# Expert weights paired into 2 MB transfers of 16 KB rows, the expert sum kept in the stream's tile, gathered rows in a tile of their own

## The chip, the cores and the metric

The kernel runs on one core of one Trainium2 chip. The metric is the device time of one execution in microseconds (us). Within a profile, times count from the start of the profiled span.

## The reference

A two-layer backbone on 256 latent tokens of width 1024 (and 256 context tokens in the first layer), all in float32. Layer 0 is attention and a dense SwiGLU; layer 1 is a short gated convolution and the part that this case is about, a top-2-of-8 expert SwiGLU:

```python
logits = h @ router_w;  top_vals, top_idx = lax.top_k(logits, 2)
gates = sum(one_hot(top_idx, 8) * softmax(top_vals)[..., None])       # (tokens, 8)
out = sum over e of gates[..., e:e+1] * ((silu(h @ w_gate[e]) * (h @ w_up[e])) @ w_down[e])
x = x + g2 * out
```

Each expert has 3 x 1024 x 3584 float32 weights (44 MB), so all eight are 352 MB, three quarters of what the kernel reads from HBM.

## The kernel before

Weights are read as a list of *units* (`order`), each 1 MB: 128 partitions by 2048 floats, that is one row of 8 KB for each partition. Units go into 8 KB-per-partition buffers that are used in a ring (`ring`, `spare()` at line 62, `load()` at line 66); the DMA is issued on the SP queue (line 68). SP issues in program order, so a buffer that is not yet free holds up every load behind it. By the expert stage the ring has 13 buffers: five of `raw1`, three of `raw2`, three of `raw3`, one of `raw4`, one of `raw5`. Two more tiles take one unit each early on (`extra`): `xhat` takes the sixth expert unit and later becomes the expert sum `macc`, and `late` takes the eleventh and is then given to the output tiles `ys`.

An expert has 7 *chunks* of 512 hidden columns. A chunk takes six units: gate and up of the first half of the input, gate and up of the second half, and, one chunk later, two units of the down projection. Experts are ranked by their number of tokens. The four with the most are *heavy*: up to 128 rows, and each weight unit is split into a high and a low part (`parts`, lines 71 to 77: ScalarE writes `hi` at line 75, VectorE writes `lo` at line 76), which are multiplied in three float32r matmuls (`mac`, lines 305 to 309). The other four are *light*: up to 64 rows, units are used as they landed, by float32 matmuls on column pairs (`pair`, line 1371). The order of chunks (`chunks`, line 92) is four heavy ones, then heavy and light in turn, then four light ones at the end.

The helper `ahead` (line 141) asks for units up to eight ahead of the one in use, splitting heavy ones some parts early, in program order on ScalarE and VectorE; so these engines wait for a transfer before they go on to later work. Work around an expert's start and end is put at steps of a chunk by `hook(chunk, step, ...)` (from line 1405): `choice` compares token ranks with slots (line 1276), `slots` transposes that (line 1336), `fetch_rows` gathers the expert's token rows from the DRAM copy `xd` by an indirect DMA on the POOL queue (line 1284) into a ring buffer taken with `spare()`, `turn_rows` transposes them on TensorE (line 1298), `output` scales an expert's result and splits it into `yh` and `yl` (lines 1381 to 1384), `scatter` multiplies it by the one-hot rows (line 1391), and `scattered` adds it to `macc` (line 1398). The first expert takes its rows from `x` directly.

Of the kernel before, what the change touches and what calls it, by code (L numbers as in the profile page):

```python
# [15 lines left out]
D = 1024  # L16
# [18 lines left out]
def trunk(ctx, tc, i, out, dbg=None):  # L35
# [10 lines left out]
    small = ctx.enter_context(pool("small", 2))  # L46
    raw1 = ctx.enter_context(pool("raw1", 5))
    cur = {}
# [10 lines left out]

    ring = [raw1] * 5  # L60

    def spare():
        ring.append(ring.pop(0))
        return ring[-1].tile([128, 2048], F32, name="raw")

# [28 lines left out]

    def weights(m, r, c, h):
        def ap():
            if r and r not in who:
                who[r] = nc.values_load(cur["who"][0:1, r:r + 1], engines=[mybir.EngineType.SP], min_val=0, max_val=NE - 1)
            return i[m][who[r] if r else 0, c, h]
        return ap  # L100

    whole += [False] * len(order)
    for n in range(len(chunks) + 1):
        if n < len(chunks):
            order += [weights(m, *chunks[n], h) for h in range(2) for m in ("moe_g", "moe_u")]
            whole += [chunks[n][0] >= NE - NL] * 4
        if n:
            order += [weights("moe_d", *chunks[n - 1], h) for h in range(2)]
            whole += [chunks[n - 1][0] >= NE - NL] * 2
# [6 lines left out]
    ready, at, used = {}, [0, None], [0]  # L116

    def feed(upto):
        while at[0] <= min(upto, most[0]):
            u, h = divmod(at[0], 2)  # L120
            if h == 0:
                src = order[u]() if callable(order[u]) else order[u]
                if u in extra:
                    at[1] = extra.pop(u)()
                    sp.dma_start(at[1], src)
                else:
                    at[1] = load(src)
# [868 lines left out]
    ph = mctx.enter_context(pool("ph", 2))  # L996
    raw2 = ctx.enter_context(pool("raw2", 3, side="right"))
    m1 = ctx.enter_context(pool("m1", 1, side="right"))
# [4 lines left out]
    dump("x1", x)  # L1003
    ring[:0] = [raw2] * 3

# [39 lines left out]

    extra[FIRST + 5] = lambda: mp.tile([128, NT, D], F32, name="xhat").rearrange("p t d -> p (t d)")

# [16 lines left out]
    for j in range(4):  # L1064
# [23 lines left out]
        if j == 3:  # L1088
            late.close()
            raw3 = ctx.enter_context(pool("raw3", 3, side="right"))  # L1090
            raw4 = ctx.enter_context(pool("raw4", 1, side="right"))
            lp = late.enter_context(pool("late", 1, side="right"))

            def join(p):
                ring.append(p)
                return p.tile([128, 2048], F32, name="raw")
# [95 lines left out]
    mctx.close()  # L1192
    raw5 = ctx.enter_context(pool("raw5", 1))
    ring += [raw5]
    me = ctx.enter_context(pool("me", 2))
# [177 lines left out]
    def output(E, q):  # L1373

        if "y" not in cur:
            late.close()
            cur["y"] = ctx.enter_context(pool("ys", 2, side="right"))
# [15 lines left out]
    def scattered(E, q, t):  # L1393
        c = slice(512 * q, 512 * q + 512)
        if "macc" not in cur:
            cur["macc"] = mp.tile([128, NT, D], F32, name="xhat")
# [13 lines left out]
    for r, E in enumerate(experts):  # L1410
# [113 lines left out]

    macc = cur["macc"]
    for s in range(4):
        down(last, s)
    y = raw1.tile([128, 2048], F32, name="raw")[:, 0:512]
    dve.scalar_tensor_tensor(y, E.accs[0], E.gs, g2l, op0=OP.mult, op1=OP.mult)
# [4 lines left out]
    for t in range(NT):  # L1534
        for q in range(2):
            c = slice(512 * q, 512 * q + 512)
            dve.tensor_add(macc[:, t, c], macc[:, t, c], ends[q, t])
            sp.dma_start(out[t * 128:(t + 1) * 128, c], macc[:, t, c])

# [4 lines left out]
    with tc.If(flag > 0):  # L1544
        spill(tc, i, out, load, pm, acc, me, m1, x, macc, rs, am, bm, pos, gts, cap, g2, iota, ident)


def spill(tc, i, out, load, pm, acc, me, m1, x, macc, rs, am, bm, pos, gts, cap, g2, iota, ident):
    nc = tc.nc
    pe, act, dve, sp = nc.tensor, nc.scalar, nc.vector, nc.sync  # L1550
    p2 = m1.tile([128, NT, NE], F32, name="p2")
    for t in range(NT):
        dve.tensor_sub(p2[:, t], pos[:, t], cap)
    for e in range(NE):
# [18 lines left out]
        for c in range(NFC):  # L1573
            pg, pu = pm(), pm()
            for half in range(2):
                for n, p in (("moe_g", pg), ("moe_u", pu)):
                    w = load(i[n][e, c, half])
                    for k in range(4):
# [10 lines left out]
            for half in range(2):  # L1589
                w = load(i["moe_d"][e, c, half])  # L1590
                for s in range(2):
# [48 lines left out]
def layout(x, c, ctx, c_ctx, ada_w, ada_b, norm1_g, norm2_g, attn_w_in, attn_w_out, qnorm_a, knorm_a, qnorm_b,  # L1640
# [37 lines left out]
    a["conv_o"] = tall(conv_w_out[0])  # L1678
    for n, w in (("moe_g", moe_w_gate), ("moe_u", moe_w_up)):
        w = np.asarray(w).reshape(NE, 2, 4, 128, NFC, FC).transpose(0, 4, 1, 3, 2, 5)  # L1680
        a[n] = A(w).reshape(NE, NFC, 2, 128, 2048)
    w = np.asarray(moe_w_down).reshape(NE, NFC, 2, 2, 128, D).transpose(0, 1, 2, 4, 3, 5)
    a["moe_d"] = A(w).reshape(NE, NFC, 2, 128, 2048)
    return a
# [15 lines left out]
```

## Time and profile before

| | |
|---|---|
| median of 3 runs | 1363.53 us (1361.49 to 1364.81) |
| the profiled execution | 1361.22 us, of which the span is 1359.4 us |
| PE (TensorE matmul) busy | 1310.8 us, 96% |
| VectorE busy | 858.4 us, 63% |
| ScalarE busy | 700.8 us, 52% |
| mean granted clock of TensorE | 0.993 of full speed |
| DMA | 473.37 MB, mean 348 GB/s over the span |

A busy PE is not a PE at its peak, since matmuls overlap. The DMA share in a row of the stretches is the mean busy share of the 16 DMA engines; a little over 1 means that their packets overlap. The expert stage runs from about 490 us to the end.

### The profile page before, as it was taken

How to read it: one execution, taken by the hardware profiler on the slowest of the kernel's cores; microseconds unless marked ns; L12 is line 12 of the kernel's file. 1: busy time of each engine (PE TensorE's matmuls, PEld its weight loads, DVE VectorE, ACT ScalarE, POOL GpSimd, SP SyncE). 2: the span in 40 equal slices, each digit the busy share in tenths (PEclk: the TensorE clock that was granted, in tenths of full speed). 3: DMA queues.
4: the chain of work that ended last, by engine and by line, in shares of the span. 5: the costliest groups of instructions: out<-in, count | busy, mean ns of one | idle time of the engine just before them, and what ended most of it. 6: DMA issues, size and time to landing. Idle time of an engine off the chain costs nothing.

```text
span 1359.4 us, 19330 instructions
## 1 busy us (share of the span) xinstructions
PE 1310.8 (96%) x7328; PEld 916.1 (67%) x7328; DVE 858.4 (63%) x1164; ACT 700.8 (52%) x975; POOL 8.2 (1%) x13
## 2 busy tenths in 40 slices
PE   6998999999999999999999999999999999999997
PEld 4766789999989987865556656655556656655532
DVE  4777758577768669865655565565555565556421
ACT  5566765444464258855545544654444644554410
POOL 0000000000000000000000000000000000000000
PEclk9999999999999989999999999999999999999999
DMA  9833769678749469699999999999999999999996
GB/s 378 293 124 101 276 268 351 244 279 310 279 171 338 174 269 385 255 422 420 420 421 420 409 421 421 404 420 420 421 404 421 407 422 419 420 408 421 421 419 254
DMA packets 67091, 473.37 MB, mean 348 GB/s; under 512 B 7472, under 2 KB 8112, under 8 KB 11056
## 3 DMA queue, kind: packets, MB, share of 16 engines
q1 hardware_dynamic: 66240, 469.46, 86.1%
q0 software_dynamic: 752, 2.62, 0.6%
q8 instruction: 59, 0.97, 0.3%
q14 instruction: 40, 0.33, 0.1%
HBM read 469.95 MB, written 2.10 MB: 347 GB/s over the span
## 4 chain that ended last, share of the span: by engine, by line
PE 78%; DMA 9%; DVE 6%; ACT 4%; issue 2%; SPq 0%; ACTq 0%; DVEq 0%
PE pm L1371 14%; DMA raw<-in_moe_g_dram 7%; PE acc L305 6%; PE acc L307 6%; PE acc L309 6%; PE pm L305 5%; PE pm L307 5%; PE pm L309 5%; PE acc L1371 5%; PE pm L961 4%; PE pm L963 4%; PE pm L962 4%; DVE lo L76 3%; DMA raw<-in_moe_d_dram 2%; PE pm L1351 2%
## 5 line engine op out<-in xcount | busy, mean ns | idle before, releaser
L76 DVE TENSOR_TENSOR lo<-raw,hi 128x1024 fp32r<-128x1024 f32 x438 | 524.8, 1223 | 180.5 <-ACT hi L75 163.0
L75 ACT ACTIVATE hi<-raw 128x1024 fp32r<-128x1024 f32 x438 | 452.8, 1058 | 251.7 <-DMA raw<-in_moe_d_dram 75.5
L1371 PE MATMUL pm<-raw,hl 128*64 128x512 f32 x896 | 207.5, 600 | 3.5 <-DVE xhat L1398 3.2
L305 PE MATMUL pm<-hi,eh 128*128 128x512 f32 x448 | 179.0, 400 | 0.2 <-ACT g L291 0.2
L307 PE MATMUL pm<-lo,eh 128*128 128x512 f32 x448 | 175.5, 392 | 2.1 <-DVE lo L76 2.0
L309 PE MATMUL pm<-hi,el 128*128 128x512 f32 x448 | 174.6, 390 | 0.0
L1371 PEld LDWEIGHTS pm<-raw,hl 128*64 128x64 f32 x896 | 60.3, 137 | 116.1 <-issue 108.2
L963 PE MATMUL pm<-th,lo 128*128 128x256 f32 x480 | 135.9, 283 | 0.0
L962 PE MATMUL pm<-tl,hi 128*128 128x256 f32 x480 | 135.6, 283 | 0.0
L961 PE MATMUL pm<-th,hi 128*128 128x256 f32 x480 | 135.6, 283 | 0.0
L1371 PE MATMUL acc<-raw,dT 128*64 128x512 f32 x448 | 103.9, 599 | 0.0
L307 PEld LDWEIGHTS pm<-lo,eh 128*128 128x128 f32 x448 | 84.2, 188 | 20.5 <-DVE lo L76 4.5
L305 PEld LDWEIGHTS pm<-hi,eh 128*128 128x128 f32 x448 | 84.1, 188 | 19.8 <-issue 0.7
L1365 DVE TENSOR_TENSOR sg<-pm,sg 128x512 f32<-128x512 f32 (+1 forms) x56 | 38.6, 690 | 92.4 <-ACT sg L1364 92.1
L309 PEld LDWEIGHTS pm<-hi,el 128*128 128x128 f32 x448 | 84.1, 188 | 17.8
L961 PEld LDWEIGHTS pm<-th,hi 128*128 128x128 f32 x480 | 91.2, 190 | 0.8 <-issue 0.4
L962 PEld LDWEIGHTS pm<-tl,hi 128*128 128x128 f32 x480 | 91.0, 190 | 0.4
L963 PEld LDWEIGHTS pm<-th,lo 128*128 128x128 f32 x480 | 91.1, 190 | 0.0
L1364 ACT ACTIVATE sg<-pm 128x512 f32<-128x512 f32 (+1 forms) x56 | 32.8, 586 | 99.4 <-PE pm L1371 97.1
L305 PE MATMUL acc<-hi,dh 128*128 128x512 f32 x224 | 72.2, 403 | 0.0
L307 PE MATMUL acc<-lo,dh 128*128 128x512 f32 x224 | 69.3, 391 | 0.0
L309 PE MATMUL acc<-hi,dl 128*128 128x512 f32 x224 | 69.1, 390 | 0.0
(331 smaller groups left out, 1525.0 us busy)
## 6 DMA issues: line engine op xcount, KB each, us to landing
raw<-in_moe_d_dram SPq DMA_DIRECT2D x112, 1024.0 KB, 14.4
raw<-in_moe_g_dram SPq DMA_DIRECT2D x111, 1024.0 KB, 14.4
raw<-in_moe_u_dram SPq DMA_DIRECT2D x111, 1024.0 KB, 14.3
raw<-in_ada_w_dram SPq DMA_DIRECT2D x48, 1024.0 KB, 6.4
raw<-in_conv_i_dram SPq DMA_DIRECT2D x12, 1024.0 KB, 6.9
raw<-in_ffn_g_dram SPq DMA_DIRECT2D x11, 1024.0 KB, 6.8
raw<-in_ffn_u_dram SPq DMA_DIRECT2D x11, 1024.0 KB, 4.9
raw<-in_ffn_d_dram SPq DMA_DIRECT2D x11, 1024.0 KB, 5.4
```

Source lines behind the costliest of these rows:

```text
L75: act.activation(hi, r, AF.Copy)
L76: dve.tensor_sub(lo, r, hi.bitcast(F32))
L305: pe.matmul(p, hh, wh[j], start=first, stop=False)
L307: pe.matmul(p, hh, wl[j], start=False, stop=False)
L309: pe.matmul(p, hl, wh[j], start=False, stop=last)
L961: pe.matmul(d, hi[:, c], th[:, k], start=(k == 0), stop=False)
L962: pe.matmul(d, hi[:, c], tl[:, k], start=False, stop=False)
L963: pe.matmul(d, lo[:, c], th[:, k], start=False, stop=(k == KD - 1))
L1351: pe.transpose(C.ps[:, k * w:(k + 1) * w], C.hd[:, k * 128:(k + 1) * 128], ident[0:w, 0:w])
L1364: act.activation(sg, C.g, AF.Silu)
L1365: dve.tensor_mul(sg, C.u, sg)
L1371: pe.matmul(ps[m * CAP:(m + 1) * CAP], lhsT, w, start=first, stop=last, tile_position=(0, m * CAP))
```

## The change

- In HBM, gate and up of a half chunk lie side by side (`moe_gu`), and so do the two down units (`moe_d`), so a pair of units is a block of 128 rows of 16 KB. `order` has a pair as one source followed by None.
- The eight `raw1` and `raw2` buffers become four pairs of places, (0,1), (2,3), (5,6) and (4,7); `raw3` is one tile of four places, which makes two pairs; the last pair is the `xhat` tile with `raw5`. For the first use, `late` stands in for `raw5`. That makes 7 pairs, 14 places. A pair whose places touch (five of the seven) is filled by one DMA of 2 MB; the two others by two DMAs of 1 MB, whose source rows of 8 KB are 16 KB apart. Both units of a pair are issued when the first of them is asked for.
- The gathered rows of an expert have a tile of their own, `xg` (one buffer), in the memory that `late` leaves; they no longer take a ring buffer. `ys` has one buffer of each of `yh` and `yl` instead of two and is allocated earlier.
- `scattered` adds into `x` itself instead of `macc`; the outputs leave from `x`. (The rare path `spill`, for too many tokens in an expert, reads the rows back from `xd`.)
- A heavy expert's second `output` moves from step 4 of the second chunk after its last one to step 1 of the third.

```diff
-    raw1 = ctx.enter_context(pool("raw1", 5))
+    raw1 = ctx.enter_context(pool("raw1", 1)).tile([128, 5 * 2048], F32, name="raw")
...
-    ring = [raw1] * 5
+    places = slots_of(raw1, *range(5))
+    ring = [*places]
+    twos = []
...
-            order += [weights(m, *chunks[n], h) for h in range(2) for m in ("moe_g", "moe_u")]
+            order += weights("moe_gu", *chunks[n], 0) + weights("moe_gu", *chunks[n], 1)
...
-            order += [weights("moe_d", *chunks[n - 1], h) for h in range(2)]
+            order += weights("moe_d", *chunks[n - 1])
...
+    def expert_unit(n):
+        if not twos:
+            last = lambda m: next(k for k, v in enumerate(ring) if v is places[m])
+            pairs = sorted([(0, 1), (2, 3), (5, 6), (4, 7)], key=lambda p: max(map(last, p)))
+            for a, b in pairs:
+                t, m = (raw1, a) if a < 5 else (cur["raw2"], a - 5)
+                twos.append([places[a], places[b]] + ([t[:, m * 2048:(m + 2) * 2048]] if b == a + 1 else []))
+        if n % 2 == 0:
+            if n // 2 in extra:
+                two = extra.pop(n // 2)()
+            else:
+                twos.append(twos.pop(0))
+                two = twos[-1]
+            src = order[FIRST + n]()
+            if len(two) == 3:
+                sp.dma_start(two[2], src)
+            else:
+                for m in range(2):
+                    sp.dma_start(two[m], src[:, m * 2048:(m + 1) * 2048])
+            cur["two"] = two
+        return cur["two"][n % 2]
...
-                src = order[u]() if callable(order[u]) else order[u]
-                if u in extra:
-                    at[1] = extra.pop(u)()
-                    sp.dma_start(at[1], src)
-                else:
-                    at[1] = load(src)
+                at[1] = load(order[u]) if u < FIRST else expert_unit(u - FIRST)
...
-    extra[FIRST + 5] = lambda: mp.tile([128, NT, D], F32, name="xhat").rearrange("p t d -> p (t d)")
...
-            for n, p in enumerate((raw3, raw3, raw3, raw4)):
-                extra[FIRST + 6 + n] = lambda p=p: join(p)
-            extra[FIRST + 10] = lambda: lp.tile([128, 2048], F32, name="late")
+            def last_two():
+                m = mp.tile([128, NT, D], F32, name="xhat").rearrange("p t d -> p (t d)")
+                twos.append([m, raw5])
+                return [lp.tile([128, 2048], F32, name="late"), m]
+
+            extra.update({3: lambda: more_twos(side(raw3, 0)), 4: lambda: more_twos(side(raw3, 2)), 5: last_two})
...
-        E.xg = spare()[0:w, 0:D]
+        if "xg" not in cur:
+            late.close()
+            cur["y"] = ctx.enter_context(pool("ys", 1, side="right"))
+            cur["xg"] = ctx.enter_context(pool("xg", 1, side="right"))
+        E.xg = cur["xg"].tile([128, D], F32, name="xg")[0:w]
...
-        macc = cur["macc"]
-        dve.tensor_add(macc[:, t, c], (x if E is experts[0] else macc)[:, t, c], E.ps)
+        dve.tensor_add(x[:, t, c], x[:, t, c], E.ps)
...
-                hook(end + 2, (1, 4)[q], output, E, q)
+                hook(end + 2 + q, 1, output, E, q)
```

## Rows read from the trace of the kernel before

**Rows 1.** The page's chain that ended last: shares by engine, then by line.
```profile
PE 78%; DMA 9%; DVE 6%; ACT 4%; issue 2%; SPq 0%; ACTq 0%; DVEq 0%
```
**Rows 2.** Busy time by stretch, columns as the first line says.
```profile
core 0: us, PE busy (x) PEld busy (x) DVE busy (x) ACT busy (x) POOL busy (x), PEclk, DMA share, GB/s
525.00:582.00 57.00, 55.13 (x263) 45.21 (x262) 50.85 (x53) 46.35 (x55) 1.85 (x1) 1.00 0.81 302
728.50:757.00 28.50, 28.50 (x130) 17.48 (x130) 16.60 (x15) 13.75 (x16) 0.00 (x0) 1.00 1.01 421
```
**Rows 3.** Chain in order of time: start, length, what; the same step one chunk pair apart.
```profile
702.62 3.58 PE acc L1371 x16
...
730.97 3.58 PE acc L1371 x16
```
**Rows 4.** Busy time by stretch, around the four starts of light experts.
```profile
640.00:668.00 28.00, 26.99 (x127) 16.09 (x124) 16.56 (x18) 16.74 (x25) 0.00 (x0) 1.00 1.02 420
...
757.00:785.00 28.00, 26.58 (x124) 15.76 (x123) 16.62 (x18) 15.68 (x19) 0.91 (x1) 1.00 1.01 406
785.00:814.00 29.00, 27.49 (x124) 15.55 (x123) 17.47 (x20) 12.56 (x14) 0.00 (x0) 1.00 1.01 419
...
970.00:998.00 28.00, 25.55 (x120) 14.91 (x119) 15.15 (x17) 14.95 (x18) 0.91 (x1) 1.00 1.01 402
998.00:1027.00 29.00, 27.85 (x126) 15.89 (x125) 18.14 (x20) 12.64 (x16) 0.00 (x0) 1.00 1.01 420
...
1184.00:1212.00 28.00, 25.64 (x111) 14.51 (x110) 14.47 (x16) 13.52 (x17) 0.91 (x1) 0.94 1.01 404
```
**Rows 5.** Chain in order of time, two of its transfers at light starts.
```profile
773.46 16.26 DMA raw<-in_moe_d_dram
...
1171.27 19.59 DMA raw<-in_moe_g_dram
```
**Rows 6.** Waits of PE, 582 to 1212 us: total us, times, longest.
```profile
PE pm L1336 <- DVE oh L1276: 6.2, 3, 2.4
PE pm L1371 <- DVE xhat L1398: 3.2, 3, 1.1
```
**Rows 7.** DMA packets and the hardware queue's share: 3:30, then 15:30, then 700:757.
```profile
DMA packets 2283, 10.96 MB, mean 406 GB/s; under 512 B 248, under 2 KB 636, under 8 KB 1635
q1 hardware_dynamic: 2282, 10.95, 100.1%
...
DMA packets 1454, 6.12 MB, mean 408 GB/s; under 512 B 167, under 2 KB 551, under 8 KB 1179
q1 hardware_dynamic: 1453, 6.11, 100.5%
...
DMA packets 3290, 23.97 MB, mean 421 GB/s; under 512 B 366, under 2 KB 366, under 8 KB 366
q1 hardware_dynamic: 3288, 23.94, 101.1%
```
**Rows 8.** Waits of the SP queue, 582 to 1330 us: total us, times, longest.
```profile
SPq L68 <- PE pm L1298: 33.4, 5, 8.5
```
**Rows 9.** Busy time by stretch, where SP stood behind the gathered rows of heavy experts.
```profile
862.00:872.00 10.00, 10.00 (x49) 6.75 (x48) 3.52 (x5) 7.27 (x14) 0.00 (x0) 1.00 0.92 361
1075.00:1085.00 10.00, 10.00 (x49) 6.13 (x46) 3.13 (x5) 6.34 (x13) 0.00 (x0) 1.00 0.96 379
```
**Rows 10.** The page's DMA issues: KB each, median us to landing.
```profile
raw<-in_moe_d_dram SPq DMA_DIRECT2D x112, 1024.0 KB, 14.4
```
**Rows 11.** Busy time by stretch, early heavy chunks.
```profile
530.00:535.00 5.00, 3.37 (x19) 2.63 (x17) 5.00 (x7) 3.32 (x5) 0.00 (x0) 1.00 0.90 320
562.00:576.00 14.00, 14.00 (x69) 11.38 (x68) 13.11 (x13) 12.19 (x14) 0.00 (x0) 1.00 0.54 194
```
**Rows 12.** The end: transfers still running by stretch, then PE's last large block.
```profile
1343.00:1344.00 1.00, 1.00 (x10) 0.37 (x6) 0.00 (x0) 0.00 (x0) 0.00 (x0) 1.00 0.46 188
...
1343.95 4.51 PE L1371 MATMUL acc<-raw,dT 128*64 128x512 f32 x20
```

More of the change, by code (lines that the diff above doesn't have):

```diff
@@ L58, in dump, with slots_of @@
             sp.dma_start(dbg[name], ap)
-    ring = [raw1] * 5
+    def slots_of(t, *ns):
+        return [t[:, n * 2048:(n + 1) * 2048] for n in ns]
+    places = slots_of(raw1, *range(5))
+    ring = [*places]
+    twos = []
     def spare():
-        ring.append(ring.pop(0))
-        return ring[-1].tile([128, 2048], F32, name="raw")
+        r = twos or ring
+        r.append(r.pop(0))
+        return r[-1][0] if twos else r[-1]
     def load(src, n=2048):
@@ L93, in trunk, with weights @@
     who, whole = {}, []
-    def weights(m, r, c, h):
+    def weights(m, r, c, *h):
         def ap():
@@ L98, in ap @@
                 who[r] = nc.values_load(cur["who"][0:1, r:r + 1], engines=[mybir.EngineType.SP], min_val=0, max_val=NE - 1)
-            return i[m][who[r] if r else 0, c, h]
-        return ap
+            return i[m][(who[r] if r else 0, c, *h)]
+        return [ap, None]
     whole += [False] * len(order)
@@ L996, in trunk @@
     ph = mctx.enter_context(pool("ph", 2))
-    raw2 = ctx.enter_context(pool("raw2", 3, side="right"))
+    raw2 = ctx.enter_context(pool("raw2", 1, side="right"))
     m1 = ctx.enter_context(pool("m1", 1, side="right"))
@@ L1003, in trunk @@
     dump("x1", x)
-    ring[:0] = [raw2] * 3
+    cur["raw2"] = raw2 = raw2.tile([128, 3 * 2048], F32, name="raw")
+    places += slots_of(raw2, *range(3))
+    ring[:0] = places[5:]
     ffn = [[acc() for _ in range(2)] for _ in range(NT)]
@@ L1089, in trunk, with side, more_twos @@
             late.close()
-            raw3 = ctx.enter_context(pool("raw3", 3, side="right"))
-            raw4 = ctx.enter_context(pool("raw4", 1, side="right"))
+            raw3 = ctx.enter_context(pool("raw3", 1, side="right")).tile([128, 4 * 2048], F32, name="raw")
             lp = late.enter_context(pool("late", 1, side="right"))
-            def join(p):
-                ring.append(p)
-                return p.tile([128, 2048], F32, name="raw")
-            for n, p in enumerate((raw3, raw3, raw3, raw4)):
-                extra[FIRST + 6 + n] = lambda p=p: join(p)
-            extra[FIRST + 10] = lambda: lp.tile([128, 2048], F32, name="late")
+            def side(t, n):
+                return [*slots_of(t, n, n + 1), t[:, n * 2048:(n + 2) * 2048]]
+            def more_twos(two):
+                twos.append(two)
+                return two
+            def last_two():
[3 more added lines that the diff above has]
+            extra.update({3: lambda: more_twos(side(raw3, 0)), 4: lambda: more_twos(side(raw3, 2)), 5: last_two})
         if j in (1, 3):
@@ L1192, in trunk @@
     mctx.close()
-    raw5 = ctx.enter_context(pool("raw5", 1))
-    ring += [raw5]
+    raw5 = ctx.enter_context(pool("raw5", 1)).tile([128, 2048], F32, name="raw")
     me = ctx.enter_context(pool("me", 2))
@@ L1373, in output @@
     def output(E, q):
-        if "y" not in cur:
-            late.close()
-            cur["y"] = ctx.enter_context(pool("ys", 2, side="right"))
         y = me.tile([128, 512], F32, name="sg", bufs=1)
@@ L1394, in scattered @@
         c = slice(512 * q, 512 * q + 512)
-        if "macc" not in cur:
-            cur["macc"] = mp.tile([128, NT, D], F32, name="xhat")
-        macc = cur["macc"]
-        dve.tensor_add(macc[:, t, c], (x if E is experts[0] else macc)[:, t, c], E.ps)
+        dve.tensor_add(x[:, t, c], x[:, t, c], E.ps)
     hooks = {}
@@ L1523, in trunk @@
     ends = {(q, t): pm() for q in range(2) for t in range(NT)}
-    macc = cur["macc"]
     for s in range(4):
         down(last, s)
-    y = raw1.tile([128, 2048], F32, name="raw")[:, 0:512]
+    y = spare()[:, 0:512]
     dve.scalar_tensor_tensor(y, E.accs[0], E.gs, g2l, op0=OP.mult, op1=OP.mult)
@@ L1536, in trunk @@
             c = slice(512 * q, 512 * q + 512)
-            dve.tensor_add(macc[:, t, c], macc[:, t, c], ends[q, t])
-            sp.dma_start(out[t * 128:(t + 1) * 128, c], macc[:, t, c])
+            dve.tensor_add(x[:, t, c], x[:, t, c], ends[q, t])
+            sp.dma_start(out[t * 128:(t + 1) * 128, c], x[:, t, c])
     manual.close()
@@ L1544, in trunk, with spill @@
     with tc.If(flag > 0):
-        spill(tc, i, out, load, pm, acc, me, m1, x, macc, rs, am, bm, pos, gts, cap, g2, iota, ident)
-def spill(tc, i, out, load, pm, acc, me, m1, x, macc, rs, am, bm, pos, gts, cap, g2, iota, ident):
+        spill(tc, i, out, load, pm, acc, me, m1, twos.pop(0)[0], xd, x, rs, am, bm, pos, gts, cap, g2, iota, ident)
+def spill(tc, i, out, load, pm, acc, me, m1, rows, xd, macc, rs, am, bm, pos, gts, cap, g2, iota, ident):
     nc = tc.nc
     pe, act, dve, sp = nc.tensor, nc.scalar, nc.vector, nc.sync
+    x = rows.rearrange("p (t d) -> p t d", t=NT)
+    for t in range(NT):
+        sp.dma_start(x[:, t], xd[t * 128:(t + 1) * 128, :])
     p2 = m1.tile([128, NT, NE], F32, name="p2")
@@ L1575, in spill @@
             for half in range(2):
-                for n, p in (("moe_g", pg), ("moe_u", pu)):
-                    w = load(i[n][e, c, half])
+                for n, p in enumerate((pg, pu)):
+                    w = load(i["moe_gu"][e, c, half][:, n * 2048:(n + 1) * 2048])
                     for k in range(4):
@@ L1589, in spill @@
             for half in range(2):
-                w = load(i["moe_d"][e, c, half])
+                w = load(i["moe_d"][e, c][:, half * 2048:(half + 1) * 2048])
                 for s in range(2):
@@ L1678, in layout @@
     a["conv_o"] = tall(conv_w_out[0])
[L1679 to L1683, printed above, removed]
+    w = np.stack([np.asarray(w).reshape(NE, 2, 4, 128, NFC, FC) for w in (moe_w_gate, moe_w_up)])
+    a["moe_gu"] = A(w.transpose(1, 5, 2, 4, 0, 3, 6)).reshape(NE, NFC, 2, 128, 4096)
+    w = np.asarray(moe_w_down).reshape(NE, NFC, 4, 128, D).transpose(0, 1, 3, 2, 4)
+    a["moe_d"] = A(w).reshape(NE, NFC, 128, 4096)
     return a
```

## The prediction

> **What bounds the kernel now.** I read the page first: PE is on 78% of the chain that ended last, the transfers on 9% [rows 1]. That is an average over several stages, so I went to the expert stage by stretches. While four or five heavy chunks run alone, the transfers idle a fifth of the time (DMA share 0.81) and VectorE is the busiest helper, 50.85 of 57 us [rows 2]: the buffers are full and consumption sets the pace. Once heavy and light chunks alternate, the DMA share is 1.01 at 421 GB/s while PE has no idle time either (28.50 of 28.50) [rows 2]. PE and the transfers are nearly level there. PE needs 28.35 us for a heavy and a light chunk, from one acc block at 702.62 to the same one at 730.97 [rows 3]; their 12 units are 12.58 MB, which take 29.9 us at 421 GB/s. So the lead of the transfers shrinks by 1.5 us each time, and is won back at the starts of light experts, where PE stalls: 1.01, 1.42 and 1.51, 2.45 and 1.15, 2.36 us idle in the six stretches, 9.9 us together [rows 4]. The last one also costs clock: the mean granted clock of its stretch is 0.94, between the levels of 2.4 and 1.2 GHz, behind PE's idle time; 28 x 0.06 = 1.7 us. Shortage in all: 11.6 us. The chain puts a transfer at these places (16.26 us from 773.46, 19.59 us from 1171.27) [rows 5]. PE waits there for VectorE by name, 6.2 us for the one-hot of L1276 [rows 6], because that operation stands behind splits that wait for those units. After 1191 us the chain shows no transfer of weights: PE runs on to the end. When the last weights are landing (188 GB/s left at 1343) PE is just about to start its last block at 1343.95 [rows 12].
>
> Hence what the change can win is PE's wait for bytes up to 1191 us, not the stream's whole saving.
>
> **Joined transfers.** The cost of a packet beside its bytes is not shown directly, but stretches with different packet sizes bound it. From 700 to 757 us the 16 engines spend 57 x 16 x 1.011 = 922.0 us on 3288 packets and 23.94 MB. From 15 to 30 us it is 241.2 us for 1453 packets and 6.11 MB. Scaled by 3.918 to equal bytes, that is 945.1 us and 5693 packets: 23.1 us for 2405 packets more, 9.6 ns each. From 3 to 30 us the same working (432.4 us, 2282 packets, 10.95 MB, factor 2.186) gives 23.4 us for 1701 packets, 13.8 ns [rows 7]. I take 11.7 ns, their mean. A 1 MB unit is 8 data packets and one short one on each engine, so a pair has 18 and lasts 2 x 2.49 = 4.98 us at 421 GB/s. As one transfer of 16 KB rows it has 9: 9 x 11.7 = 0.105 us less, 4.88 us. No row has packets above 8 KB, so the ends are zero (rows still cut into 8 KB packets) and 13.8 ns; a loss of the same size, rows of 16 KB moving worse, is not excluded, though the rate rises with packet size (406 and 408 to 421 GB/s [rows 7]). Five pairs of seven are joined: 0.075 us a pair on average, 1.5%. From about 590 us, where the stream becomes the bound, to 1191 us there are 601 / 4.98 = 121 pairs: **9.0 us** of DMA time (7.4 to 10.8, or zero).
>
> The trace shows a 1 MB unit landing 14.4 us after its issue [rows 10], but units follow each other every 2.49 us, so the fixed part of a transfer is hidden behind the five in the queue. The Trainium skill, "DMA: Bandwidth & Descriptors", section "Anatomy of one DMA", gives a fixed cost of about 2.0 us for each DMA beside its bytes; paid in full, the 86 joins up to 1191 us would save 172 us. The rate of 421 GB/s leaves no room for that, so the rows decide, and it does not enter the sum.
>
> **What joining costs.** The first unit of a joined pair now lands with the second, half a pair later: 2.44 us. The transfers that end the stalls are first units (a gate unit, a first down unit [rows 5]), so PE's shortage grows by **2.4 us** once; not at every start, since the stream itself is not slowed by who waits for it. Issue does not get later. A pair is issued when the pair seven before is free, and its second unit was that which freed the 13th buffer back before; the second unit of the new pair goes out earlier than it did. SP issues one DMA instead of two.
>
> **Rows in a tile of their own.** Before, the gathered rows held a ring buffer, and SP stood behind the transposes that free it (L1298) for 33.4 us in five waits, the longest 8.5 us [rows 8]. Mostly the queue of 14.4 us [rows 10] covers that. At the starts of two heavy experts it ran dry: 361 and 379 instead of 421 GB/s for 10 us each [rows 9], (60 + 42) / 421 x 10 = **2.4 us** of transfer time returned. At 562 to 576 us the DMA share is 0.54 with PE full [rows 11]; there consumption bounds, so I count nothing (bound: one unit more of lead, 2.5 us). On POOL nothing is queued behind the gather that has a deadline; `xg` needs the memory of `late`, consumed before the first gather.
>
> **Output and sum.** PE waits 3.2 us in three places for L1398 [rows 6], each in the second chunk after a heavy expert's end, where VectorE and ScalarE do two outputs beside the splits. One of them moves a chunk on, before the scatter that uses it and, with single `yh` and `yl`, after the scatters of the first half, a chunk earlier. Between 0 and 3.2 us; I take half, **1.6 us**. The accumulator it reads is kept a chunk longer, but the next heavy expert asks for one seven steps later. Adding into `x` is the same number of additions; cover: the copy of `x` to `xd` is done hundreds of microseconds before the first of them.
>
> **Early chunks.** From 490 to 535 us the stream is short too: PE has 3.37 of 5 us at 530 while VectorE is at 5.00 [rows 11]. First units landing 2.44 us later, less 45 us x 1.5% = 0.7, cost up to 1.7 us; the extra lead above would pay for it. I take **1.0 us** lost.
>
> **The sum.** Shortage 11.6 - 9.0 - 2.4 + 2.4 = 2.6 us left, so 9.0 us won; plus 1.6, minus 1.0: 9.6 us. The profiled execution took 1361.2 us (span 1359.4 and 1.8 around it), 2.3 us below the median of 1363.5, and the gain is the same for both: 1351.6 and, for the median, 1353.9, say **1354**. With the ends of the terms: shortage left 0.8 to 4.2 us, outputs 0 to 3.2, early 0 to 1.7 lost, that is 5.7 to 14 us, 1349.5 to 1358. More than about 15 us is not there: PE's idle time and lost clock before 1212 us are the cap.
>
> **Rivals.**
> (1) *The packet's own cost is small, or rows of 16 KB are cut up.* Then only one short packet in 18 goes, 5/7 x 11.7 ns = 8 ns a pair, 1.0 us; own tile and later landing cancel, and outputs less early loss leave about 1 us: 1362. For it: no packet above 8 KB in the trace, and my 11.7 ns is a small difference of large sums. Against it: two stretches agree. The Trainium skill says much the same in "DMA: Bandwidth & Descriptors", section "Why small descriptors are slow": some 3 cycles for each packet beside one for 32 bytes, and joining only worth it up to 256 bytes; by that estimate 8 KB has 256 + 3 and a doubled row saves 0.6%, some 2.5 us up to 1191, which gives 1360. The packets of 4 to 5 KB on average [rows 7] are slower than it allows. Chance 0.18.
> (2) *PE's stalls are order, not bytes.* If the one-hot and the outputs are late because ScalarE and VectorE reach them late, a faster stream wins only what the outputs and a part of the stalls give, 3 us: 1360.5. For it: PE names VectorE [rows 6]. Against it: the chain goes on to transfers [rows 5]. Chance 0.14.
> (3) *Landing together becomes a new stall at each light start.* This decides if the stream itself runs dry there: pairs are asked for in bursts, and if SP stands longer than the queue of 14.4 us [rows 10], the DMA share falls below 1 and the 2.44 us are paid four times, 9.8 us, less 2 us from the outputs: 1371. The point is a stand of about 14.4 us; the longest at the old rows was 8.5 us [rows 8], which speaks against it. Slower moving rows of 16 KB would give the same side (up to 9 us). Chance 0.14.
>
> **How the numbers follow.** Forecast 0.54, rivals 0.18, 0.14, 0.14. A measurement can tell about 0.3%, 4.1 us, from no change, so faster means below 1359.4. Nearly all of the forecast (0.53) and a part of rivals 1 and 2 (0.08) lie there: 0.61; the most of these two, 0.25, is the same; rival 3 is slower, 0.14. The range runs from 1347, where the cap of 15 us bites, to 1365, which takes in rivals 1 and 2 and leaves rival 3 out.
>
> **What would show it.** In the profile after: stretches of the alternating chunks at about 427 GB/s (421 refutes the first term), packets of 16 KB, so about 2000 in place of 3290 for as many bytes; no SP wait for L1298; no drop to 361 GB/s at heavy starts; PE idle time at light starts well below 9.9 us; L1398 off PE's waits. A DMA share below 1 at light starts would be rival 3. The prediction is wrong if the rate rises and PE's idle time does not shrink.

## The result and the profile after

The changed kernel takes 1353.59 us (median of 4 runs, 1351.35 to 1356.45) beside 1362.88 us for the kernel before, a ratio of 0.9932 [0.9908, 0.9956]. That is 9.3 us less, between 6.0 and 12.5 by the interval; predicted were 1354 us and 9.6 us less. The profiled execution of after took 1356.45 us, the slowest of its four.

The page of after first: the count of packets, the chain's shares by engine, and the two large DMA issues of expert weights (count, KB each, median us to landing).

```profile
DMA packets 49808, 473.34 MB, mean 349 GB/s; under 512 B 5552, under 2 KB 6192, under 8 KB 9136
...
PE 84%; DMA 5%; DVE 5%; ACT 3%; issue 1%; SPq 0%; ACTq 0%; DVEq 0%
...
raw<-in_moe_gu_dram SPq DMA_DIRECT2D x80, 2048.0 KB, 14.5
raw<-in_moe_d_dram SPq DMA_DIRECT2D x40, 2048.0 KB, 15.4
```

The transfers' share of the chain fell from 9 to 5% [rows 1]. A transfer of 2 MB lands hardly later after its issue than one of 1 MB did (14.5 and 15.4 us beside 14.4, [rows 10]), so about as many bytes stand in the queue as before. Next the packets of 700 to 757 us, then busy time by stretch (columns as in [rows 2]).

```profile
DMA packets 2102, 24.28 MB, mean 426 GB/s; under 512 B 236, under 2 KB 236, under 8 KB 236
```
```profile
525.00:582.00 57.00, 55.09 (x255) 45.11 (x254) 49.37 (x52) 44.91 (x53) 1.84 (x1) 0.97 0.98 392
728.50:757.00 28.50, 28.50 (x130) 17.52 (x129) 16.93 (x16) 14.67 (x16) 0.00 (x0) 1.00 1.01 427
757.00:785.00 28.00, 28.00 (x131) 16.98 (x130) 15.29 (x18) 14.66 (x18) 0.90 (x1) 1.00 1.00 401
970.00:998.00 28.00, 26.74 (x126) 15.65 (x126) 16.96 (x18) 15.16 (x19) 0.90 (x1) 1.00 1.01 405
1184.00:1212.00 28.00, 26.09 (x120) 15.54 (x117) 15.43 (x18) 14.12 (x18) 0.90 (x1) 0.94 1.01 403
850.00:880.00 30.00, 29.45 (x136) 17.74 (x135) 17.11 (x18) 18.81 (x27) 0.06 (x1) 1.00 1.01 424
```

2102 packets in place of 3290 [rows 7], 427 GB/s in place of 421 [rows 2], no drop around the start of a heavy expert ([rows 9]; the stretch of 850 to 880 us moved 402 GB/s before and moves 424). PE's idle time in the six stretches of [rows 4] is 4.0 us instead of 9.9, most of it at the third and fourth start of a light expert. The unexpected line is the first: the early heavy chunks now move 392 GB/s, where the DMA share was 0.81 at 302 [rows 2]. Last, PE's waits from 582 to 1212 us, and the chain's longest transfers.

```profile
PE pm L1371 <- DVE oh L1307: 3.2, 2, 1.9
PE pm L333 <- DVE lo L84: 1.6, 3, 0.5
PE pm L1333 <- ACT xg L1323: 0.5, 1, 0.5
```
```profile
954.78 19.63 DMA raw<-in_moe_gu_dram
...
985.88 20.24 DMA raw<-in_moe_gu_dram
...
1165.35 20.28 DMA raw<-in_moe_gu_dram
```

The wait for the one-hot halved (L1307 was L1276) and the one for the sum (L1398) is gone [rows 6]; SP waits 0.9 us for the transposes of the gathered rows instead of 33.4 [rows 8]. These are the third and fourth light start; at the second, where before had one [rows 5], the chain shows no transfer now.

### Two ways to read where the time went

*PE's place*: the time at which a chunk's transposes begin on PE (the line of `pe.transpose(C.ps`, 1351 in before, 1386 in after), less the same in before, with the difference at chunk 3 (571.78 us in before) set to zero. Up to chunk 3 the profiled executions differ from that of before by up to 4.4 us, and executions of one kernel among themselves (after 4.36, a2 1.84); 1.5 us of it is told below, the rest lies ahead of the expert stage and stays open.

| kernel (one profile each) | chunk 14, 737 us | 28, 951 us | 43, 1179 us | 46, 1227 us | 55, 1344 us |
|---|---|---|---|---|---|
| after | -1.2 | -5.8 | -9.2 | -9.6 | -9.6 |
| after again (a2) | -1.2 | -5.8 | -4.8 | -8.8 | -8.8 |
| e1: pairs as two DMAs | -1.8 | -6.4 | -7.5 | -6.9 | -6.9 |
| e3: before, own tile | -1.8 | -3.9 | -4.3 | -3.2 | -3.1 |
| e4: before, output moved | -0.9 | -0.4 | -0.1 | +0.2 | +0.2 |
| e14: e3 with a 14th place | -1.8 | -6.4 | -6.0 | -6.3 | -6.3 |
| e8b: after, look-ahead of 5 | -1.9 | -6.5 | -11.5 | -15.6 | -13.7 |
| e13: e8b, pairs as two DMAs | -1.8 | -6.4 | -11.1 | -15.1 | -7.3 |
| e9: before, look-ahead of 5 | -1.8 | -3.0 | -5.1 | -9.1 | -2.6 |

*The stream's place* (the stream is the row of weight transfers on the SP queue) at the fourth light start: when ScalarE's splits (L75, L83) start that waited for a transfer. Before, two down units and the gate unit behind them:

```profile
1186.02 2.01 ACT L75 ACTIVATE hi<-raw 128x1024 fp32r<-128x1024 f32 x2 [5.38 <-DMA raw<-in_moe_d_dram]
1188.50 2.01 ACT L75 ACTIVATE hi<-raw 128x1024 fp32r<-128x1024 f32 x2 [0.47 <-DMA raw<-in_moe_d_dram]
...
1190.97 1.06 ACT L75 ACTIVATE hi<-raw 128x1024 fp32r<-128x1024 f32 x1 [0.47 <-DMA raw<-in_moe_g_dram]
```
After:
```profile
1180.81 3.90 ACT L83 ACTIVATE hi<-raw 128x1024 fp32r<-128x1024 f32 x4 [4.97 <-DMA raw<-in_moe_d_dram]
1185.74 1.06 ACT L83 ACTIVATE hi<-raw 128x1024 fp32r<-128x1024 f32 x1 [1.03 <-DMA raw<-in_moe_gu_dram]
```

Before, units come 2.48 us apart; after, both down units are there at once and the gate unit comes 4.93 us later, with its pair. From chunk 3 on (after's trace is 4.36 us late there) the down pair is complete at 1180.81 - 4.36 = 1176.45 instead of 1188.50: **the stream is 12.05 us ahead**. The gate unit, on which PE's next work hangs, is 1190.97 - (1185.74 - 4.36) = **9.59 us** ahead, since 2.46 us go to landing together. PE gained 9.61 us. So the path of the prediction holds: at the last light start PE's place is the stream's place, and afterwards PE runs to the end without a stall. That the two agree to 0.02 us is luck: in the second execution of after (a2) the gate unit is 8.00 us ahead and PE 8.8. And PE's tie to the gate unit goes through the order of work on VectorE, as an experiment below shows.

### The profile page after: what moved, and what is told of

It is laid out like the page before. It is cut to its first block, busy times and chain, and to the rows that moved or that the text cites. A ratio compares the mean times of both kernels' runs of the same rounds, so it can differ in the third digit from the quotient of the medians.

```text
span 1354.6 us, 18815 instructions
## 1 busy us (share of the span) xinstructions
PE 1313.7 (97%) x7328; PEld 918.9 (68%) x7328; DVE 858.4 (63%) x1164; ACT 700.7 (52%) x975; POOL 9.1 (1%) x13
## 4 chain that ended last, share of the span: by engine, by line
PE 84%; DMA 5%; DVE 5%; ACT 3%; issue 1%; SPq 0%; ACTq 0%; DVEq 0%
PE pm L1406 14%; PE acc L331 7%; PE acc L333 7%; PE acc L335 7%; PE pm L331 6%; PE acc L1406 6%; PE pm L333 6%; PE pm L335 6%; DMA raw<-in_moe_gu_dram 4%; PE pm L989 4%; PE pm L987 4%; PE pm L988 4%; PE pm L1386 2%; DVE lo L84 2%; PE pm L1423 1%
## 5 line engine op out<-in xcount | busy, mean ns | idle before, releaser
L84 DVE TENSOR_TENSOR lo<-raw,hi 128x1024 fp32r<-128x1024 f32 x418 | 500.4, 1222 | 154.1 <-ACT hi L83 138.4
L83 ACT ACTIVATE hi<-raw 128x1024 fp32r<-128x1024 f32 x418 | 432.3, 1058 | 227.9 <-PE pm L988 69.2
L1400 DVE TENSOR_TENSOR sg<-pm,sg 128x512 f32<-128x512 f32 (+1 forms) x56 | 38.6, 689 | 93.2 <-ACT sg L1399 92.9
L1406 PE MATMUL acc<-raw,dT 128*64 128x512 f32 x408 | 94.6, 599 | 0.0
## 6 DMA issues: line engine op xcount, KB each, us to landing
raw<-in_moe_gu_dram SPq DMA_DIRECT2D x80, 2048.0 KB, 14.5
raw<-in_moe_d_dram SPq DMA_DIRECT2D x40, 2048.0 KB, 15.4
xhat<-in_moe_gu_dram SPq DMA_DIRECT2D x16, 1024.0 KB, 12.5
```

The lines of the kernel that those rows point to most:

```text
L83: act.activation(hi, r, AF.Copy)
L84: dve.tensor_sub(lo, r, hi.bitcast(F32))
L1400: dve.tensor_mul(sg, C.u, sg)
L1406: pe.matmul(ps[m * CAP:(m + 1) * CAP], lhsT, w, start=first, stop=last, tile_position=(0, m * CAP))
```

## The experiments

Theory: the stream of weights is what PE waits for, and rows of 16 KB are most of what it gains. Rivals: a packet costs less than thought, and the gain comes from places and tiles; or the stalls are the order of work on VectorE.

**The price of a packet by itself.** A kernel that only loads blocks of 2 MB, 48 for each form, through eight buffers:

```diff
+    def rows16(n):
+        sp.dma_start(two(), gu[n])
+    def rows8_one(n):
+        sp.dma_start(two().rearrange("p (n c) -> p n c", n=2), gu[n:n + 2, :, 0:2048].rearrange("n p c -> p n c"))
...
+    for stage in (rows4, rows8, rows8_flat, rows8_one, rows16, rows16_halves, rows16):
```

> Computes nothing; it streams the experts' gate and up weights seven times over, 48 blocks of 2 MB each time, in seven forms one after the other: (1) four transfers of 4 KB rows, (2) two of 8 KB rows that lie 16 KB apart, (3) two of 8 KB rows that lie side by side, (4) one transfer of 2 MB in 8 KB rows, (5) one transfer of 16 KB rows, (6) two transfers of 64 partitions in 16 KB rows, (7) form 5 again. The theory (each packet costs some 8 ns beside its bytes; that is the 421 to 425.5 GB/s of the changed kernel, five pairs in seven joined): forms 2 and 3 at 421, form 4 at 422, form 5 at 427 to 428, form 6 at 427, form 1 at 409 GB/s. The first rival (the cost is one of the transfer, some 74 ns, not of the packet): form 4 at 427 as form 5, form 6 at 421. The second rival (the rate does not depend on the form, the changed kernel's gain in rate came from the order of its loads): all forms within 1 GB/s of each other.

Stretches of it (columns: us from start to end, length, POOL's busy time, granted clock, DMA share, GB/s): rows of 4 KB; two of 8 KB, 16 KB apart; two of 8 KB side by side; one DMA of 2 MB with rows of 8 KB; rows of 16 KB; 16 KB in two halves of 64 partitions.

```profile
30.00:270.00 240.00, 0.00 (x0) 1.00 1.03 411
280.00:500.00 220.00, 0.00 (x0) 1.00 1.01 422
510.00:730.00 220.00, 0.00 (x0) 1.00 1.01 422
740.00:960.00 220.00, 0.00 (x0) 1.00 1.01 422
970.00:1190.00 220.00, 0.00 (x0) 1.00 1.01 428
1200.00:1420.00 220.00, 0.00 (x0) 1.00 1.01 215
```

2.097 MB take 4.970 us at 422 GB/s and 4.900 at 428, with 9 packets fewer on each engine: 7.7 ns a packet; from 4 to 8 KB it is 5.103 to 4.970 us for 18, 7.4 ns. The stride in HBM and the size of a DMA make no difference at equal rows: it is the packet that costs. The prediction took 11.7 ns. One expectation missed: the halves of 64 partitions were expected at 427 GB/s and move at 215.

The Trainium skill, "DMA: Bandwidth & Descriptors", section "Why small descriptors are slow", counts some 3 cycles a packet beside one for 32 bytes; by an estimate from that, doubling an 8 KB row would save 0.6%. The rows show 1.4% (422 to 428).

**Pairs as two DMAs.** All of the change but the rows of 16 KB:

```diff
-            if len(two) == 3:
+            if False:
```

> The changed kernel with every joined pair filled by two transfers of 1 MB with 8 KB rows; places, order of issue and the tile of the gathered rows stay. The theory (the longer rows give the rate): alternating chunks back at 421 GB/s, the light starts lose 601 us x 1.2% = 7.1 us and get back up to 2.4 us since first units land earlier: 1358 us, 4 to 5 us slower than the changed kernel. The rival (places, order and the rows' own tile did it all): 1353.6 us, as the changed kernel, with its PE idle times.

1353.67 us (1352.95 to 1355.69), 0.9921 [0.9904, 0.9937]: as fast as after, not 1358. The rate is back at 421 GB/s (728.5 to 757). Its splits at the fourth light start:

```profile
1178.43 2.01 ACT L83 ACTIVATE hi<-raw 128x1024 fp32r<-128x1024 f32 x2 [5.97 <-DMA raw<-in_moe_d_dram]
1180.93 2.00 ACT L83 ACTIVATE hi<-raw 128x1024 fp32r<-128x1024 f32 x2 [0.49 <-DMA raw<-in_moe_d_dram]
1183.42 1.06 ACT L83 ACTIVATE hi<-raw 128x1024 fp32r<-128x1024 f32 x1 [0.48 <-DMA raw<-in_moe_gu_dram]
```

With 0.66 us for its earlier chunk 3, the stream is 1188.50 - 1181.59 = 6.9 us ahead of before, without any row of 16 KB. So these rows are worth 12.05 - 6.9 = 5.1 us of stream and, less the 2.46 us of landing together, 2.7 us of PE's time. Other traces bear this out: by the same working the stream is 11.9 to 12.8 us ahead in four more executions with these rows (e6, e8, e8b, e11 below) and 6.8 us in one without them (e13), so 5 to 6 us; a2 alone, at 10.44, would make it 3.5. The times can't show so little: their intervals are 2.2 us (e1) and 3.3 us (after) wide on each side.

**The own tile and the output, without pairs.** The kernel before with `xg`, single `ys` and the moved output:

```diff
-        E.xg = spare()[0:w, 0:D]
+        E.xg = cur["xg"].tile([128, D], F32, name="xg")[0:w]
...
-                hook(end + 2, (1, 4)[q], output, E, q)
+                hook(end + 2 + q, 1, output, E, q)
```

> The kernel before, with two parts of the change alone: the gathered rows in a tile of their own (with single yh and yl), and a heavy expert's second output a chunk later; units stay single 1 MB transfers in the ring. The theory: the three waits behind L1398 go (3.8 us) and 2.4 us of transfer time come back at the heavy starts, no loss in the early chunks: about 1357 us. The rival (the rows' tile gives nothing, the queue covers SP's stand): 1359 us. If 16 KB rows were all there is: 1363 us.

and with the second of these edits alone:

> The kernel before with only the second output of a heavy expert moved a chunk later. The theory: three waits of about 1.25 us each go, 3.8 us, 1359 us; the profile has no PE wait for L1398. The rival (the stream sets the end, so what PE gains here it loses at the next light start): 1363 us, with the light starts' idle time grown by what the waits gave.

The first takes 1357.82 us (1357.07 to 1361.45), 0.9954 [0.9937, 0.9971]; the second 1367.41 us (1361.56 to 1369.23), 1.0008 [0.9996, 1.002], no change. PE's waits in the second:

```profile
PE pm L1336 <- DVE oh L1276: 7.8, 3, 2.7
...
PE pm L1371 <- DVE xhat L1398: 0.4, 1, 0.4
```

The wait for L1398 falls from 3.2 to 0.4 us and the one for the one-hot grows from 6.2 to 7.8 [rows 6]: PE gets 1.3 us earlier at each heavy end and waits longer at the next light start, where the stream is what is late. The output's term is worth nothing while bytes are short. So the theory for the first kernel met its number (1357) by a wrong sum: 3.8 us of it were the output's. The own tile does bring something. Bytes landed from the start to 611 us (shifted by each trace's own chunk 3), before and then e3:

```profile
DMA packets 24236, 166.77 MB, mean 273 GB/s; under 512 B 2687, under 2 KB 3327, under 8 KB 5183
```
```profile
DMA packets 24425, 168.18 MB, mean 275 GB/s; under 512 B 2704, under 2 KB 3344, under 8 KB 5200
```

1.41 MB more have landed, more than one unit (1.05 MB), before the stream becomes the bound. Where they come from, the waits of SP and the stretches of 562 to 590 us show. SP's wait for the transposes of the gathered rows in before (540 to 600 us; e4, with the output alone moved, has the same one, e3 has none), a stretch of before, then two of e3:

```profile
SPq L68 <- PE pm L1298: 11.5, 1, 11.5
```
```profile
572.00:576.00 4.00, 4.00 (x25) 3.14 (x24) 3.66 (x4) 3.60 (x5) 0.00 (x0) 1.00 0.01 4
```
```profile
562.00:576.00 14.00, 14.00 (x69) 11.37 (x68) 13.10 (x13) 12.18 (x14) 0.00 (x0) 1.00 1.02 397
586.00:590.00 4.00, 4.00 (x22) 1.37 (x20) 2.26 (x3) 1.16 (x2) 0.00 (x0) 1.00 0.02 8
```

In before SP stood for 11.5 us behind the first gathered rows, longer than any wait of [rows 8], which begin at 582 us, and the queue ran dry (4 GB/s, where e3 has 410); then it issued six units within 3.2 us, into buffers that had been free. That is the DMA share of 0.54 in [rows 11]; e3, at the same pace of PE, moves 397 GB/s there. At 586 to 590 us e3 is at rest, as its buffers are full; before runs at full rate from there on and does not make up the difference. The landing times of single units put e3 3.2 us ahead at 617 us and 3.3 us at 1188: the lead is taken once, early, and kept. At the two heavy starts of [rows 9] e3 gains about 0.9 us each time (3.2 to 4.1 and 3.1 to 4.1 us ahead) and has lost most of it again by the next light start.

**A 14th place without pairs.** e3 with the sum in `x` and the `xhat` tile kept in the ring:

```diff
-    extra[FIRST + 5] = lambda: mp.tile([128, NT, D], F32, name="xhat").rearrange("p t d -> p (t d)")
+    extra[FIRST + 5] = lambda: keep(Kept())
...
-        dve.tensor_add(macc[:, t, c], (x if E is experts[0] else macc)[:, t, c], E.ps)
+        dve.tensor_add(x[:, t, c], x[:, t, c], E.ps)
```

> The kernel before with the rows' own tile, the moved output, the sum kept in x, and the xhat tile as a 14th buffer of the ring; units stay single 1 MB transfers, each asked for by itself. The theory (what the pairs as two transfers won beyond the rows' own tile, 3.8 us between the fourth chunk and the end, is the 14th place): 3 to 4 us better than the rows' own tile alone, 1354 us. The rival (it is that both units of a pair go out at once): 1357.8 us, as with the rows' own tile alone.

1357.66 us (1356.76 to 1359.47), 0.9943 [0.9931, 0.9956]. By time alone it stands where e3 stands. Its trace says otherwise: bytes landed by 611 us, then the second down unit at the fourth light start of e3, then of e14.

```profile
DMA packets 24574, 169.27 MB, mean 276 GB/s; under 512 B 2720, under 2 KB 3360, under 8 KB 5216
```
```profile
1185.09 2.00 ACT L75 ACTIVATE hi<-raw 128x1024 fp32r<-128x1024 f32 x2 [0.48 <-DMA raw<-in_moe_d_dram]
```
```profile
1185.15 2.00 ACT L75 ACTIVATE hi<-raw 128x1024 fp32r<-128x1024 f32 x2 [0.48 <-DMA raw<-in_moe_d_dram]
```

One place more is 1.09 MB more by 611 us (169.27 to 168.18), so that e14 has as much there as e1 (169.23). With chunk 3 at -0.07 and +2.95 us, the streams are 3.3 and 6.3 us ahead of before: the 14th place is worth 3.0 us of stream, as long as one unit takes and a little, and PE's place ends at -6.3 instead of -3.1. The rest up to e1's 6.9, 0.6 us, may be the issue by pairs, but two traces don't tell so little apart. That the time of e14 does not show the 3 us is in part chance: its profiled execution, the median one, was 2.95 us late at chunk 3 already, e3's 0.07 us early. By the intervals its gain on e3 is 1.5 us, give or take 2.9; so the 3 us are shown by the traces and not by the times.

**After once more**, for the scatter of a trace:

> The changed kernel unaltered, timed beside the next three and profiled once more. The theory (it is 0.7% faster; its first profile was 3.1 us late already in the first 50 us, by chance): ratio 0.992 to 0.994, and a profile in which the chunks from the fourth on lie 9 to 10 us better against the kernel before than the fourth itself. The rival (the offset of the early chunks belongs to the change): the same 3 to 4 us late at the first chunk.

1355.64 us (1352.36 to 1357.84), 0.9926 [0.9908, 0.9944]. PE's place ends at -8.8. At the third light start this execution lost some 4 us more than after's first one (-4.8 beside -9.2 at chunk 43), most of it clock: behind 2.0 us of idle time the granted clock was 0.54 from 976 to 982 us and 0.89 to 988, 3.4 us, where after's first execution has 1.00. At the fourth it has no idle time and is back near it: the stream was ahead there of the later PE. Its own place is 10.44 us ahead instead of 12.05: in 1075 to 1106 and 1106 to 1136 us it moved 413 and 414 GB/s where after had 427 and 423, and why stays open.

**Order instead of bytes.** At the fourth light start of after, VectorE reaches the one-hot (L1307) behind splits of units that have only just landed:

```profile
1181.90 4.63 DVE L84 TENSOR_TENSOR lo<-raw,hi 128x1024 fp32r<-128x1024 f32 x4 [5.06 <-ACT hi L83]
1186.82 1.23 DVE L84 TENSOR_TENSOR lo<-raw,hi 128x1024 fp32r<-128x1024 f32 x1 [0.29 <-ACT hi L83]
1188.08 0.69 DVE L1400 TENSOR_TENSOR sg<-pm,sg 128x512 f32<-128x512 f32 x1
1188.69 0.47 DVE L1307 TENSOR_SCALAR oh<-cst,posr 128x128 f32<-128x128 f32 x2
```

A shorter look-ahead in `ahead` lets these operations go first; it is applied to after, to before, and in a still shorter form:

```diff
-        while split and k <= most[0] and k // 2 - n // 2 < 9:
+        while split and k <= most[0] and k // 2 - n // 2 < 6:
```

> The changed kernel with one number altered: a split is put into the order of ScalarE and VectorE at most 5 units ahead of the one in use, not 8. Nothing else moves; the loads wait for places, not for this. The theory (PE's stalls at light starts are splits of units 6 to 8 ahead that stand in front of the one-hot and the hidden rows while their transfer is under way; the bytes themselves would still be in time): PE's 3.5 us at the last two light starts and 1.7 us of clock go, 1348.5 to 1350 us. The rival (bytes are short): the stalls return at the splits' own users, 1353.6 us. Worse than both, if splits now come too late in the alternating chunks: 1360 us.

> The kernel before with the same one number altered. The theory: its stalls at light starts (9.9 us and 1.7 us of clock) go as well, but the stream then ends later than PE (the last weights land at 1343 us against PE's end at 1349), so about 5 us are kept: 1358 us. The rival (bytes are short): 1363 us, no change.

> The changed kernel with splits at most 4 units ahead. With 5 units one stall of 2 us is left (1212 to 1245 us: an output stands behind a split whose pair is under way). The theory: it goes too, 2 us better than with 5 units, about 1350 us. The rival (splits now come too late, PE waits for VectorE's lo part at each heavy chunk behind a light one): each of some 24 chunks loses part of a microsecond, 1355 us or more.

> The changed kernel with splits at most 5 units ahead, once more beside the others. The theory (4 us less between the fourth chunk and the end than the changed kernel, as in its first profile): 1350 to 1352 us, ratio 0.989 to 0.991.

On after: 1352.25 us (1349.13 to 1353.25), 0.9906 [0.9891, 0.9921], and when run again 1351.33 us (1350.39 to 1351.58), 0.9895 [0.9881, 0.9909]. Both medians lie below those of the two kernels. With `< 5` it is 1354.27 us (1349.89 to 1354.78), 0.9909 [0.9895, 0.9924], no better by time, which is the rival's number. In its trace the last stall is gone, as the theory had it (33.00 of 33.00 us busy from 1212 to 1245, PE's place ends at -15.5), but it was 4.2 us late at chunk 3; times and trace don't decide between the two. On before it is 1362.56 us (1358.4 to 1364.42), 0.9978 [0.9966, 0.9989]: 3 us, between the rival (no change) and the theory (5 us). The stretches of the second run on after:

```profile
757.00:785.00 28.00, 28.00 (x130) 16.95 (x130) 16.70 (x18) 15.45 (x19) 0.90 (x1) 1.00 1.01 402
970.00:998.00 28.00, 28.00 (x135) 17.37 (x132) 17.42 (x20) 13.69 (x18) 0.90 (x1) 1.00 1.01 402
1184.00:1212.00 28.00, 28.00 (x131) 17.50 (x133) 16.47 (x18) 14.89 (x19) 0.90 (x1) 1.00 1.01 405
1212.00:1245.00 33.00, 31.48 (x136) 18.14 (x134) 20.21 (x22) 16.23 (x19) 0.00 (x0) 1.00 1.01 426
```

No idle time is left at a light start; one stall of 1.5 us comes behind the last. On before, PE's place follows to -9.1 at 1227 us and falls back to -2.6: PE runs up to the bytes there and stops. The waits at the light starts of after were order; take the order away in before, and the bytes stop PE one chunk later.

**The same with pairs as two DMAs**, which asks what rows of 16 KB are worth once order is out of the way (`< 6` and `if False`):

> The changed kernel with splits at most 5 units ahead and every joined pair filled by two transfers of 1 MB with 8 KB rows. The theory (16 KB rows are worth what PE still waits for bytes): without them the stream is 7 us later by the last light start, and PE, which then waits for it again, loses 2 to 4 us against the same kernel with joined pairs: 1355 us. The rival (with the look-ahead cut PE has slack, the rows are worth nothing): 1352.3 us.

1356.17 us (1353.5 to 1358.45), 0.9931 [0.9917, 0.9945], beside 0.9895 and 0.9906 with them. The transfer that ends the last stall, here and then with rows of 16 KB (e8b), from the chains; then busy time of PE here in two stretches (us, PE, granted clock, DMA share, GB/s):

```profile
1198.93 19.77 DMA raw<-in_moe_gu_dram
```
```profile
1191.31 23.83 DMA raw<-in_moe_gu_dram
```
```profile
1218.00:1224.00 6.00, 1.66 (x6) 0.88 1.01 421
1224.00:1230.00 6.00, 6.00 (x16) 0.55 1.01 419
```

It lands at 1218.70 instead of 1215.14 us (chunk 3 within 0.1 us of each other), so 16 KB rows bring it 3.6 us forward, landing together included. PE's place falls by 7.8 us here, by 1.9 in e8b: 4.3 us of idle time and 6 x 0.12 + 6 x 0.45 = 3.4 us of clock, at 0.88 and 0.55 between the levels of 2.4 and 1.2 GHz, behind it. The rows of 16 KB decide 3.4 to 4.9 us of the time (0.9931 less 0.9906 or 0.9895, each give or take 2.8 us); by PE's place it is 6.4 us here (-13.7 beside -7.3), where after and e1 differ by 2.7.

**The one-hot earlier**, in after:

```diff
-            hook(n - 3, 10, choice, E, posr)
+            hook(n - 3, 2, choice, E, posr)
```

> The changed kernel with the one-hot of an expert (L1307) eight steps earlier in its chunk, ahead of those splits. The theory: the wait of the transposes for it (3.2 us in two places) goes, but the hidden rows (L1400) stand behind the same splits and take its place at the next step, so 0.5 to 1 us of it stays won: 1353 us. The rival (the one-hot alone is late): 3 us and the clock, 1349 us.

1354.41 us (1351.99 to 1356.31), 0.9925 [0.9907, 0.9943], no change that can be measured. The wait for the one-hot is gone, and waits for the hidden rows (L1400) come in, 3.2 us in two places up to 1330 us: they stand in the same order behind the same splits.

## Why the prediction was right, and which terms were not

The time came out 0.4 us from the forecast, and that is luck: rows of 16 KB and outputs were put 5.5 us too high, places, own tile and early chunks 5.5 us too low. The path (a faster stream shortens PE's wait for bytes at the light starts) was right. In us of PE's gain from chunk 3 on:

| step | predicted | shown by |
|---|---|---|
| rows of 16 KB, stream | +9.0 | +5.1 (after less e1) |
| landing together | -2.4 | -2.46 (gap of 4.93 instead of 2.47) |
| own tile | +2.4 | +3.3 (e3, output moved with it), from another place |
| the 14th place | 0, bound 2.5 | +3.0 (e14 less e3) |
| issue by pairs | 0 | +0.6 (what is left to e1) |
| outputs | +1.6 | 0 (e4) |
| early chunks | -1.0 | not seen |
| sum (of unrounded terms) | 9.6 | 9.6 |

The terms shown are steps of one quantity, the stream's place from trace to trace, so they add up by construction; what could have failed is that PE's place ends where the stream's does.

- *What bounds the kernel.* Right, for the order in which the work stands: PE waits for VectorE behind splits that wait for the stream, as the prediction says. The gate unit is 9.59 us ahead and PE 9.61. In before the bytes themselves are short as well: with the shorter look-ahead PE stops for them one chunk later.
- *Joined transfers.* Right in kind, too large. The price of 11.7 ns came from early stretches with rows of 2 KB and below among others; alone it is 7.7. 86 joined pairs of 9 x 7.7 ns are 6.0 us, where the streams show 5.1 (5 to 6 in the other traces, 3.5 in a2). The lower end of the range (7.4 us) lay above it: two stretches that agree did not make a bound. The forecast of 427 GB/s held for a stretch without a gather; the mean from 611 to 1184 us is 422, beside 419 in e1.
- *What joining costs.* Right, paid once. It makes 5.1 us of stream 2.7 us of time.
- *The places.* The step that failed is "there consumption bounds, so I count nothing (bound: one unit more of lead, 2.5 us)". At 562 to 576 us it was not consumption but SP, 11.5 us behind the first gathered rows; that stand cost before 1.41 MB of lead by 611 us, and a lead is kept until the stream is short. The 2.4 us that were counted, for the drops of [rows 9], left nothing by the last light start; that the own tile's +3.3 is near them is luck. The 14th place, counted as nothing too, is 1.09 MB. At 421 GB/s the two are 3.3 and 2.6 us, some 6 us in all. The rise from 302 to 392 GB/s in the early chunks is mostly the stand that is gone (e3 has 386 in the same stretch); some of it is only earlier, since by 611 us after is 2.6 MB ahead. Counting this as zero hid the overrated packet.
- *Outputs.* Wrong as a sum: the wait went as foreseen, but a gain of PE ahead of a stall by bytes is given back there. In after's trace the 1.3 us at each heavy end are not given back at the next start, but as PE's place ends at the stream's, they add nothing to the sum.
- *Early chunks.* The shift of 1.5 us between chunks 0 and 3 that after's trace has (granted clock 0.97 in 525 to 582) is there in e3, e14, e4 and e9 too, which have no joined transfers, and absent in e8b and e11, which have the change (clock 1.00 from 525 to 611): it belongs to an execution, not to the change.
- *Rivals.* (1) was right on the packet's price in part (5/7 x 9 x 7.7 is 50 ns a pair on average, between its 8 and the forecast's 75), wrong on the total. (2) holds for before in small part: of its 11.6 us the shorter look-ahead frees 3 (0.9978). It holds for most of what the change left: the same edit there moves the ratio from 0.9932 and 0.9926 to 0.9906 and 0.9895, about 4 us, give or take 2.5. (3) did not come: the DMA share stays at 1.00 and 1.01 at light starts.

What stays open: the traces put single executions side by side. The profiled one of before (1361.22 us) is 4 us below the medians that the kernel had beside the experiments (1365.3 to 1365.8), so e3's gain is 3.1 us by the traces and 6.3 [4.0, 8.6] by the ratio. That the stream's steps end at PE's 9.6 us is shown for the traces; how the 9.3 us of the medians divide is known to about 3 us for each step.

## What to carry to other kernels

Where a stream falls behind slowly over a long stretch, ask what it has in its buffers when that stretch begins. A stand of the issuing engine shortly before it, even one during which TensorE is full, and a place too few in the ring each cost some 3 us here, once (a unit takes 2.5); so read the waits of the issuing engine over the stretch ahead too, before a low DMA share is put down to full buffers. Price a packet by streams that differ in nothing else; and charge a joined transfer with the later landing of its first half. When PE waits for an engine that works in program order, look at what was put ahead in that order: bytes and order hide each other, and the second shows only when the first is mended.

## What was not expected of the hardware

- A transfer of 64 of the 128 partitions moves at half the rate: 215 GB/s beside 428 with the same rows of 16 KB (the stretches of the loading kernel, where 427 were expected). Splitting a pair by partitions, so that its first half lands early, would cost the stream's rate.
- Idle time of 2 to 4 us was followed by some 6 us at about half the clock in two traces (e13: 0.55 behind 4.3 us; a2: 0.54 behind 2.0), and idle time of 2.45 us in before, in 970 to 998 us at 1.00 [rows 4], was not. Executions of one kernel differ in step with their mean clock: e4's ten lie between 1361.56 us (mean clock 0.994) and 1369.23 (0.987).
